# An encoder step on one Trainium2 core: the first branch product of the mix is traced in the front stage, in the buffers of h

## The chip, the cores and the metric

The kernel runs on one core of one Trainium2 chip. The metric is device time in microseconds (us) for one execution of the whole step. The core has five instruction queues that matter here: TensorE (PE, matmuls, with PEld for its weight loads), VectorE (DVE), ScalarE (ACT), GpSimd (POOL) and SyncE (SP), which issues nearly all DMA transfers. Each queue runs its instructions in order, and an instruction that waits for a semaphore holds everything behind it on the same queue.

## The reference, cut to what matters

One layer of a hybrid encoder runs for a prompt of 256 tokens and for eight samples of 16 tokens, together 384 token columns (NT). D is 1024.

```
mod = silu(c) W_ada + b_ada -> sh1, sc1, g1, sh2, sc2, g2
h   = RMSNorm(x) * (1 + sc1) + sh1
P   = h W_in  -> [RWKV-7 | sparse attention + indexer | two gates]
o_a = RWKV-7 time mixing           (16 heads of 64)
o_b = sparse attention:  q = rope(rmsnorm(q)), k = rope(rmsnorm(k)),
      indexer top-k selects keys, softmax over them, times v
gate_a, gate_b = sigmoid(P_gate + b_gate)
m   = gate_a * (o_a @ w_proj_a) + gate_b * (o_b @ w_proj_b)
x   = x + g1 * (m @ w_out)
h2  = RMSNorm(x) * (1 + sc2) + sh2
x   = x + g2 * PEER(h2)            (product keys: top 16 of 16384 experts)
```

The line that computes m is called the mix. Branch A is `gate_a * (o_a @ w_proj_a)`, branch B is the other product.

## The kernel before

All matmuls of interest take three products: an operand is split into a high and a low part (`hilo`, L230 on ACT for the high part, L234 on DVE for the low part), and high*high, low*high and high*low are added in one PSUM accumulator. A weight unit (`wload`) is two loads of 128x1024 from DRAM, each split in the same way. `tposp` then makes 24 matmuls (8 contraction steps k, 3 products) into one PSUM tile "mm" of 128x384. "mm" has two buffers.

The kernel is traced in program order, and a scheduler then puts each engine's instructions in an order of its own by a simulated timeline, with the trace order as the priority. What it writes is fixed before the run. Tiles come from pools; a tile with a tag waits for the last use of the tile that had its buffer before, and a new pool that lies on the room of a closed one waits for the old pool's last use of that room.

The stages, with their times in the profiled execution: modulation and h (to about 130 us); the front (to about 718 us), in which `ORDER` (L177) lists the units: index I, eight RWKV pairs R (R0 to R7), four attention quarters D (D0 to D3), the modulation units M (`w_ada`) and sixteen gate units G. M and G are the fill between the chains of R and D. Then come the mix (L1175), the four units of `w_out`, h2, the scores and selection of PEER (DVE does most there), and from about 1000 us to the end the dense expert stage.

The pieces that the change touches:

- RWKV pair e ends with three transposes of y (L674), a multiplication on DVE (L675, into tile sq) and a write of 128x384 to DRAM `oad[:, e]` (L676). An attention quarter u writes 128x2x384 to `obd` (L974) from a tile with the tag "qr". A gate unit writes its sigmoid to `gd` (L1164, tile gg).
- `mix` loads the products back. `parts` (L1166) makes the operands of one branch: four loads "px" of 128x768 (two buffers), each split into pbh/pbl (branch A) or pah/pal (branch B). Each branch then runs four weight units of two chunks, 192 matmuls of 128x384. Branch A's chunks are multiplied by the gate into ga (L1190), branch B's into gm, and the sum gm + ga (L1192, POOL) is split again as the operand of `w_out`.
- The pool of px lies where pools of the front lay, which are closed only after the front (`fh.close`).
- `rope` (L871) rotates pairs: two half multiplications by the sine table on POOL (L877, L878, tile rpt), one multiplication by the cosine table on DVE (L880), one addition on DVE (L881). It is called eleven times: twice in each quarter (K, then Q) and twice for the indexer's queries at 128x3x4x64, and once for the indexer's key at a quarter of that size.
- In `dsa_quarter`, K and Q are copied out of PSUM (L888, tile qx), squared on ACT (L947, into rpt), reduced on DVE (L949), turned into a reciprocal root on POOL (L436, qss), multiplied with it on DVE (L951), rotated by `rope` into kr (tag "qr"), and transposed on PE (L959).
- `attend_p` (L1063) does the prompt's part of a quarter in two halves i=0, i=1: QK and mask matmuls ("dx" accumulators), maximum on DVE (L1080), exp on ACT (L1084, tile se), transposes of it (L1092), its product with v (`dx<-vv,set`), and the transposes of the result (L1105). All its PSUM tiles have the tag "dx", which has two buffers.
- h's operand pair LTh, LTl lies in the pool hpool, one buffer each; the units that multiply with `w_in` (those of R, D and G) read it to the end of the front.

Of the kernel before, what the change touches and what calls it, by code (L numbers as in the profile page):

```python
# [13 lines left out]
F32R = mybir.dt.float32r  # L14
# [159 lines left out]

PSB = {"mm": 2, "fx": 2, "bx": 1, "dx": 2, "cp": 1}
ALIAS = {"ix": "cp", "cs": "bx", "u": "fx"}
ORDER = "GGIggggR1R23DMMMGRMRDMRGMGMRMDGMMRRMGDMMMGGGMGGM"  # L177


N1, NW, NA, NB = 40, 76, 8, 24  # L180
# [15 lines left out]
class K:  # L196
# [338 lines left out]
    def rwkv_pair(self, e):  # L535
# [137 lines left out]
        for i in range(3):  # L673
            nc.tensor.transpose(p[:, i], y[:, i], self.ident)  # L674
        nc.vector.tensor_tensor(oq, oq, p.rearrange("p i t -> p (i t)"), op=OP.mult)  # L675
        nc.sync.dma_start(self.oad[:, e], oq)  # L676
    def rwkv_inverse(self, e, MBs, MBp):


# [191 lines left out]
    def rope(self, dst, x, which, n):  # L871

        nc = self.nc
        tab = self.rt[:, which]
        B = lambda j: tab[:, :, j].unsqueeze(2).to_broadcast([128, 3, n, 32])
        t = self.t([128, 3, 4, 64], tag="rpt")[:, :, :n]
        nc.gpsimd.tensor_tensor(t[:, :, :, 0:32], x[:, :, :, 32:64], B(2), op=OP.mult)  # L877
        nc.gpsimd.tensor_tensor(t[:, :, :, 32:64], x[:, :, :, 0:32], B(3), op=OP.mult)  # L878
        cc = tab[:, :, 0:2].rearrange("p i a b -> p i (a b)").unsqueeze(2).to_broadcast([128, 3, n, 64])
        nc.vector.tensor_tensor(dst, x, cc, op=OP.mult)  # L880
        nc.vector.tensor_tensor(dst, dst, t, op=OP.add)  # L881
# [50 lines left out]
    def dsa_quarter(self, u):  # L932
        nc = self.nc
        H = lambda t: t.rearrange("p i (h d) -> p i h d", d=64)
        cols = slice(u * 256, (u + 1) * 256)
        qTs = self.t([128, 2, 8, 2, 16], tag="qTs")
        nc.gpsimd.memset(qTs, 0.0)
        qTp = self.t([128, 2, 2, 256], tag="qTp")
        for par in range(2):
            nc.gpsimd.memset(qTp[64 - 64 * par:128 - 64 * par, par], 0.0)  # L940
        kT = self.t([128, 2, NT], tag="kT")
        vn = self.t([128, 3, 256], tag="vv")
        for which, nm in ((1, "K"), (0, "Q")):
            x = self.t([128, 3, 256], tag="qx")
            self.nat3(f"{nm}{u}", x, 256)
            sq = self.t([128, 3, 256], tag="rpt")
            nc.scalar.activation(sq, x, AF.Square)  # L947
            ss = self.t([128, 3, 4], tag="qss", bufs=2)
            nc.vector.tensor_reduce(out=ss, in_=H(sq), op=OP.add, axis=AX.X)  # L949
            r = self.rstd(ss, ss, 1.0 / 64, EPS)  # L950
            nc.vector.tensor_tensor(H(x), H(x), r.unsqueeze(3).to_broadcast([128, 3, 4, 64]), op=OP.mult)  # L951
            kr = self.t([128, 3, 4, 64], tag="qr")
            self.rope(kr, H(x), 1 + which, 4)
            if which == 1:
                nc.sync.dma_start(self.O["k"][:, cols].rearrange("(i p) c -> p i c", p=128), kr.rearrange("p i a b -> p i (a b)"))
            for c in range(2):
                p = self.ps([128, 3, 128], tag="dx")
                for i in range(3):
                    nc.tensor.transpose(p[:, i], kr[:, i, 2 * c:2 * c + 2].rearrange("p a b -> p (a b)"), self.ident)  # L959
                if which == 1:  # L960
                    nc.scalar.activation(kT[:, c], p.rearrange("p i t -> p (i t)"), AF.Copy)
                else:
                    pv = p[:, 0].rearrange("p (b t) -> p b t", t=16)
                    nc.scalar.activation(qTs[0:64, c, :, 0], pv[0:64], AF.Copy)
                    nc.scalar.activation(qTs[64:128, c, :, 1], pv[64:128], AF.Copy)
                    for par in range(2):
                        pr = slice(64 * par, 64 * par + 64)
                        nc.scalar.activation(qTp[pr, par, c], p[pr, 1:3].rearrange("p i t -> p (i t)"), AF.Copy)
        self.nat3(f"V{u}", vn, 256)
        nc.sync.dma_start(self.O["v"][:, cols].rearrange("(i p) c -> p i c", p=128), vn)  # L970
        ob = self.t([128, 2, NT], tag="qr")
        self.attend_s(u, qTs, kT, vn, ob)
        self.attend_p(u, qTp, kT, vn, ob)
        nc.sync.dma_start(self.obd[:, 2 * u:2 * u + 2], ob)  # L974
    def select(self, work, rounds):

        nc = self.nc
        for _ in range(rounds):
            m8 = self.t([128, 8], tag="m8", bufs=2, pool=self.hpool)
            nc.vector.max(m8, work)  # L980
            nc.vector.match_replace(out=work, in_to_replace=m8, in_values=work, imm_value=MARK)

# [24 lines left out]
    def pick_p(self, i):  # L1007
        nc = self.nc
        n, sc = 128 * (i + 1), self.isc[1 + i]
        self.select(sc[:, :n], 8)  # L1010
        mk = self.t([128, 256], BF16, tag="mkp", bufs=2, pool=self.hpool)
        nc.vector.tensor_scalar(mk[:, :n], sc[:, :n], MARK, -BIG, op0=OP.not_equal, op1=OP.mult)
        self.mkp.append(mk)

# [34 lines left out]
    def pick_s(self):  # L1049
        nc = self.nc  # L1050
        sc = self.isc[0]
        self.select(sc, 9)
        mk = self.t([128, 384], BF16, tag="mks", pool=self.hpool)
        nc.vector.tensor_scalar(mk[:, 0:256], sc[:, 0:256], MARK, -BIG, op0=OP.not_equal, op1=OP.mult)
        m2 = self.t([128, 16], tag="m2", pool=self.hpool)
        nc.vector.tensor_scalar(m2, sc[:, 256:272], MARK, -BIG, op0=OP.not_equal, op1=OP.mult)
        ob = self.t([128, 8], tag="ob8", pool=self.hpool)
        nc.vector.tensor_scalar(ob, self.c["blk"], 1.0, BIG, op0=OP.subtract, op1=OP.mult)
        nc.vector.tensor_tensor(mk[:, 256:384].rearrange("p (b t) -> p b t", t=16), m2.unsqueeze(1).to_broadcast([128, 8, 16]),
                                ob.unsqueeze(2).to_broadcast([128, 8, 16]), op=OP.min)  # L1060
# [1 line left out]

    def attend_p(self, u, qT, kT, vn, obT):  # L1063
        nc = self.nc
        for i in range(2):
            n = 128 * (i + 1)
            nk = i + 1
# [7 lines left out]
            for par in range(2):  # L1075
# [8 lines left out]
                    nc.scalar.activation(e[:, j, :n], p[:, j, :n], AF.Exp, scale=0.125, bias=mx[:, j:j + 1],  # L1084
                                         accum_out=sm[:, 2 * j + par:2 * j + par + 1])
                es.append(e)
            pv = self.ps([128, 4, 64], tag="dx")
            for par, e in enumerate(es):
                pt = self.ps([128, 2, 2, 128], tag="dx")
                for j in range(2):  # L1090
                    for kc in range(nk):
                        nc.tensor.transpose(pt[:, j, kc], e[:, j, kc * 128:(kc + 1) * 128], self.ident)  # L1092
# [7 lines left out]
            nc.vector.reciprocal(sm, sm)  # L1100
            ob = self.t([128, 4, 64], tag="ob")
            nc.vector.tensor_tensor(ob, pv, sm.unsqueeze(2).to_broadcast([128, 4, 64]), op=OP.mult)
            p = self.ps([128, 2, 128], tag="dx")
            for c in range(2):
                nc.tensor.transpose(p[:, c], ob[:, 2 * c:2 * c + 2].rearrange("p a b -> p (a b)"), self.ident)  # L1105
            nc.scalar.activation(obT[:, :, 128 + i * 128:128 + (i + 1) * 128], p, AF.Copy)
# [52 lines left out]
    def gate_unit(self, u):  # L1159
# [3 lines left out]
        self.sigmoid(g, self.tposp(W, 0, 128, self.LT), self.hb[:, 16 + u:17 + u])  # L1163
        self.nc.sync.dma_start(self.gd[u], g)  # L1164

    def parts(self, src, tag):  # L1166
        hi = self.t([128, 8, NT], F32R, tag=tag + "h")
        lo = self.t([128, 8, NT], F32R, tag=tag + "l")
        for k in range(0, 8, 2):
            x = self.t([128, 2, NT], tag="px", bufs=2)  # L1170
            self.nc.sync.dma_start(x, src[:, k:k + 2])
            self.hilo(hi[:, k:k + 2], lo[:, k:k + 2], x)
        return hi, lo

    def mix(self):  # L1175
        nc = self.nc
        I = self.I
        gb = self.t([128, 8, NT], tag="ga")
        for br, (src, w, tg) in enumerate(((self.oad, "w_proj_a", "pb"), (self.obd, "w_proj_b", "pa"))):
            LT = self.parts(src, tg)  # L1180
            if br:
                mh, ml = self.mT = [self.t([128, 8, NT], F32R, tag=tag) for tag in ("pbh", "pbl")]
            for u in range(4):
                W = self.wload(I[w][:, u], 256)
                for c in range(2):
                    k = 2 * u + c
                    g = self.t([128, NT], tag="gm", bufs=2) if br else gb[:, k]
                    nc.sync.dma_start(g, self.gd[8 * br + k])
                    p = self.tposp(W, c, 128, LT)
                    nc.vector.tensor_tensor(g, g, p, op=OP.mult)  # L1190
                    if br:
                        nc.gpsimd.tensor_tensor(g, g, gb[:, k], op=OP.add)  # L1192
                        self.hilo(mh[:, k], ml[:, k], g, eng="v")

        self.g1 = self.t([128, 2, 1024], tag="row2")
        an = self.t([128, 3, 1024], tag="pah")
# [393 lines left out]
    def run(self):  # L1590
        hs = self.ctx.enter_context(ExitStack())
        self.halves = self.open(hs, "halves")
        with ExitStack() as front:
            fh = front.enter_context(ExitStack())
            self.fconst = self.open(fh, "fconst")
            self.hpool = self.open(fh, "hpool")
            self.fill = self.open(fh, "fill")
            self.psum = self.open(self.ctx, "psum", space=bass.MemoryType.PSUM)
            self.lo_pattern = "v"
# [10 lines left out]
                    self.setup_front()  # L1610
            self.lo_pattern = "v"
            self.gd = self.dt_([16, 128, NT])
            self.oad, self.obd = self.dt_([128, 8, NT]), self.dt_([128, 8, NT])
            with ExitStack() as s:
                rw = self.open(s, "rw")
                self.pool = rw
# [3 lines left out]
                for x in ORDER:  # L1620
# [134 lines left out]
```

## Time and profile before

| | |
|---|---|
| median of three runs | 1762.96 us (1759.18 to 1770.17) |
| the profiled execution | 1759.49 us, its span 1757.7 us |
| mean granted TensorE clock of that execution | 0.981 |
| PE busy over the span | 1679.5 us (96%) |
| DVE / ACT / POOL busy | 1353.6 / 747.5 / 550.5 us |
| front, 130 to 690 us | PE busy 541.24 of 560 us, DVE 431.33, POOL 189.59 |
| branch A's first and branch B's last matmul | about 708 and 783 us |

The engines' busy times are given by window in the prediction; a window row holds, for each engine, its busy time and the number of instructions, then the granted clock (1.00 is full), the share of the DMA engines' time and the rate. A row of the timeline holds the start, the duration, the engine, the line, the operation, the output and the inputs, and in brackets how long the engine had been idle and which instruction ended that. "SPq" is a DMA issue on SyncE; the transfer goes on after it, and the group rows give the median time from issue to landing.

### The profile page before, as it was taken

The page shows a single profiled execution, that of the slowest core. Times are in us where ns is not written, and L with a number is a line of the kernel's source. Part 1 is how long each engine was busy: PE and PEld are TensorE (multiplying, and loading weights), DVE is VectorE, ACT ScalarE, POOL GpSimd, SP SyncE. Part 2 cuts the span into 40 slices and gives each one's busy share as a digit, 9 for nine tenths or more (in the row PEclk, how much of TensorE's full clock was granted, in tenths as well). Part 3 has the DMA queues.
Part 4 walks back from the last instruction along what each step waited for, and adds up shares of the span by engine and source line. Part 5 has one row for each costly group of instructions (what it writes and reads, how often), then busy time and mean ns, then how long its engine had stood idle before and what let it go on. Part 6 is the DMA issues. An engine that isn't in the chain of part 4 may idle for free.

```text
span 1757.7 us, 33129 instructions
## 1 busy us (share of the span) xinstructions
PE 1679.5 (96%) x12392; PEld 1410.2 (80%) x12392; DVE 1353.6 (77%) x2907; ACT 747.5 (43%) x1666; POOL 550.5 (31%) x616
## 2 busy tenths in 40 slices
PE   6999899999999999999998999999999999999998
PEld 4988788777888877899887889999976667767766
DVE  4448878778867765556999998899957778778787
ACT  4533343334342333335323255578853433443344
POOL 2433343333333421024032233342243224323232
PEclk8999899999999999999999999999999999999999
DMA  8543662555365365765488999997569999999996
GB/s 305 161 123 101 187 194 68 145 166 174 94 197 161 94 207 189 246 193 171 144 334 313 358 333 366 397 340 238 179 251 381 348 346 376 375 349 391 349 379 216
DMA packets 172537, 436.71 MB, mean 248 GB/s; under 512 B 46036, under 2 KB 86100, under 8 KB 155992
## 3 DMA queue, kind: packets, MB, share of 16 engines
q1 hardware_dynamic: 153944, 300.36, 50.8%
q0 software_dynamic: 18432, 134.23, 19.7%
q8 instruction: 98, 1.61, 0.4%
q14 instruction: 63, 0.52, 0.1%
HBM read 403.23 MB, written 31.30 MB: 247 GB/s over the span
## 4 chain that ended last, share of the span: by engine, by line
PE 55%; DVE 19%; DMA 11%; issue 8%; ACT 3%; POOL 2%; SPq 1%; DVEq 0%; POOLq 0%; ACTq 0%
PE mm L226 21%; PE fx L226 10%; PE dx L226 10%; PE cp L226 6%; PE bx L226 6%; DMA raw<-in_puv,pe 3%; DVE wl L234 3%; DVE raw L1580 2%; DVE acc L1586 2%; DMA w<-in_puT 2%; DMA w<-in_pv 2%; ACT wh L230 1%; DMA w<-in_w_in 1%; DVE TX L698 1%; DMA NL<-d 1%
## 5 line engine op out<-in xcount | busy, mean ns | idle before, releaser
L234 DVE TENSOR_TENSOR wl<-w,wh 128x1024 fp32r<-128x1024 f32 (+1 forms) x276 | 345.8, 1260 | 109.0 <-ACT wh L230 71.3
L230 ACT ACTIVATE wh<-w 128x1024 fp32r<-128x1024 f32 (+1 forms) x284 | 296.6, 1050 | 163.7 <-PE mm L226 74.3
L1573 POOL DMA_INDIRECT raw<-in_puv,pe x128 | 173.6, 1356 | 423.4 <-PE dx L226 155.4
L226 PE MATMUL fx<-h2h,wl 128*128 128x256 f32 x704 | 200.1, 285 | 8.2 <-DVE wl L234 8.0
L226 PE MATMUL fx<-h2h,wh 128*128 128x256 f32 x704 | 200.6, 285 | 1.4 <-ACT wh L230 1.1
L226 PE MATMUL fx<-h2l,wh 128*128 128x256 f32 x704 | 197.4, 281 | 0.0
L1586 DVE SCALAR_TENSOR_TENSOR acc<-raw,dots,acc 128x1024 f32<-128x1024 f32 x127 | 166.1, 1308 | 14.8 <-ACT dots L1582 14.8
L1580 DVE SCALAR_TENSOR_TENSOR raw<-raw,sh 128x1024 f32<-128x1024 f32 x128 | 158.9, 1241 | 14.0 <-DMA raw<-in_puv,pe 13.8
L226 PEld LDWEIGHTS fx<-h2h,wl 128*128 128x128 f32 x704 | 132.7, 189 | 12.3 <-DVE wl L234 11.5
L226 PEld LDWEIGHTS fx<-h2h,wh 128*128 128x128 f32 x704 | 132.6, 188 | 6.4 <-ACT wh L230 3.6
L226 PEld LDWEIGHTS fx<-h2l,wh 128*128 128x128 f32 x704 | 132.9, 189 | 1.6 <-issue 1.1
L226 PE MATMUL mm<-LTh,wh 128*128 128x384 f32 (+2 forms) x352 | 123.4, 351 | 1.4 <-ACT wh L230 0.8
L226 PE MATMUL mm<-LTl,wh 128*128 128x384 f32 (+2 forms) x352 | 123.1, 350 | 0.9 <-POOL LTl L488 0.9
L226 PE MATMUL mm<-LTh,wl 128*128 128x384 f32 (+2 forms) x352 | 122.4, 348 | 0.0
L226 PE MATMUL mm<-h2f,w 128*128 128x256 f32 x448 | 104.0, 385 | 0.0
L226 PE MATMUL mm<-wh,LTh 128*128 128x256 f32 x336 | 100.3, 299 | 2.9 <-ACT qx L888 2.9
L1581 ACT ACTIVATE dots<-dots 128x1 f32<-128x1 f32 x128 | 25.6, 200 | 177.0 <-DVE raw L1580 176.5
L226 PE MATMUL mm<-wl,LTh 128*128 128x256 f32 x336 | 99.4, 296 | 0.0
L226 PE MATMUL mm<-wh,LTl 128*128 128x256 f32 x336 | 98.6, 293 | 0.0
L226 PEld LDWEIGHTS mm<-h2f,w 128*128 128x128 f32 x448 | 85.0, 192 | 12.2 <-issue 0.2
L226 PE MATMUL fx<-h2f,w 128*128 128x256 f32 x320 | 73.8, 383 | 0.0
L226 PEld LDWEIGHTS mm<-LTh,wh 128*128 128x128 f32 (+2 forms) x352 | 66.5, 189 | 7.1 <-issue 3.0
(577 smaller groups left out, 4235.0 us busy)
## 6 DMA issues: line engine op xcount, KB each, us to landing
w<-in_puT SPq DMA_DIRECT2D x128, 512.0 KB, 7.1
w<-in_pv SPq DMA_DIRECT2D x128, 512.0 KB, 6.6
w<-in_w_in SPq DMA_DIRECT2D x70, 512.0 KB, 4.5
w<-in_w_ada SPq DMA_DIRECT2D x48, 512.0 KB, 4.8
cKT<-in_cKT SPq DMA_DIRECT2D x32, 256.0 KB, 4.3
cV<-in_cV SPq DMA_DIRECT2D x32, 256.0 KB, 4.5
w<-in_w_pq SPq DMA_DIRECT2D x16, 512.0 KB, 4.2
d<-wst SPq DMA_DIRECT2D x8, 832.0 KB, 4.3
```

The lines of the kernel that those rows point to most:

```text
L226: return self.nc.tensor.matmul(out, l, r, start=start, stop=stop, skip_group_check=True, **kw)
L230: self.nc.scalar.activation(hi, src, AF.Copy)
L234: (self.nc.vector if eng == "v" else self.nc.gpsimd).tensor_tensor(lo, src, hi, op=OP.subtract)
L698: nc.vector.tensor_tensor(X[:, :t, :t], T[:, :t, :t].rearrange("p s c -> p c s"), NL[:, :t, t].unsqueeze(1).to_broadcast([48, t, t]), op=O ...
L1573: d = nc.gpsimd.indirect_dma_start(out=bass.AP(tensor=u.tensor, offset=u.offset, ap=[u.ap[0], [1, 2048]]), out_offset=None, in_=self.I["puv"],
L1580: nc.vector.scalar_tensor_tensor(u, u, 1.0, h2, op0=OP.mult, op1=OP.mult, accum_out=dot)
L1581: nc.scalar.activation(dot, dot, AF.Gelu_apprx_tanh)
L1586: nc.vector.scalar_tensor_tensor(acc, v, dot, acc, op0=OP.mult, op1=OP.add)
```

## The change: what it does

1. **Branch A moves into the front.** A new function `branch_a` is traced behind the ORDER loop, before the front's pools are closed. Its operands take the tags LTh and LTl, that is h's two buffers, so that its first split waits for the last matmul that reads h. It loads o_a in eight chunks of 128x384 ("pt", two buffers, from the RWKV pool), splits each, loads the gate chunks ("Xk", two buffers of the RWKV pool), runs the 192 matmuls, multiplies (DVE) and writes eight chunks of 192 KB to new DRAM tensors `gad`. The mix loads `gad` in place of gate A, and does branch B only.
2. **Pools.** hpool is opened outside of the front's other pools and stays open until h2 is made; the mix's sum takes LTh and LTl again instead of pbh and pbl. Small tiles of the selection (m8, mkp, mks, m2, ob8) move to fconst. `oad` and `obd` become four DRAM tensors each.
3. **ORDER's tail** goes from `DMMMGGGMGGM` to `DMGMGMGMGGM`.
4. **rope and the norm.** L878's half multiplication goes from POOL to DVE. In a quarter the square goes into kr ("qr") instead of rpt, and the multiplication by the reciprocal root comes after the rotation instead of before it.
5. **The last quarter's `attend_p`** takes its PSUM tiles pt, pv and p from the tags "fx", "cp" and "bx" instead of "dx".

```diff
-ORDER = "GGIggggR1R23DMMMGRMRDMRGMGMRMDGMMRRMGDMMMGGGMGGM"
+ORDER = "GGIggggR1R23DMMMGRMRDMRGMGMRMDGMMRRMGDMGMGMGMGGM"
...
-        nc.sync.dma_start(self.oad[:, e], oq)
+        nc.sync.dma_start(self.oad[e // 2][:, e % 2], oq)
...
         nc.gpsimd.tensor_tensor(t[:, :, :, 0:32], x[:, :, :, 32:64], B(2), op=OP.mult)
-        nc.gpsimd.tensor_tensor(t[:, :, :, 32:64], x[:, :, :, 0:32], B(3), op=OP.mult)
+        nc.vector.tensor_tensor(t[:, :, :, 32:64], x[:, :, :, 0:32], B(3), op=OP.mult)
...
-            sq = self.t([128, 3, 256], tag="rpt")
-            nc.scalar.activation(sq, x, AF.Square)
+            kr = self.t([128, 3, 4, 64], tag="qr")
+            nc.scalar.activation(kr.rearrange("p i a b -> p i (a b)"), x, AF.Square)
             ss = self.t([128, 3, 4], tag="qss", bufs=2)
-            nc.vector.tensor_reduce(out=ss, in_=H(sq), op=OP.add, axis=AX.X)
+            nc.vector.tensor_reduce(out=ss, in_=kr, op=OP.add, axis=AX.X)
             r = self.rstd(ss, ss, 1.0 / 64, EPS)
-            nc.vector.tensor_tensor(H(x), H(x), r.unsqueeze(3).to_broadcast([128, 3, 4, 64]), op=OP.mult)
-            kr = self.t([128, 3, 4, 64], tag="qr")
             self.rope(kr, H(x), 1 + which, 4)
+            nc.vector.tensor_tensor(kr, kr, r.unsqueeze(3).to_broadcast([128, 3, 4, 64]), op=OP.mult)
...
     def attend_p(self, u, qT, kT, vn, obT):
         nc = self.nc
+        tags = ("fx", "cp", "bx") if u == 3 else 3 * ("dx",)
...
+    def pair_lt(self):
+        return [self.t([128, 8, NT], F32R, tag=tag, pool=self.hpool) for tag in ("LTh", "LTl")]
+
+    def branch_a(self):
+        nc = self.nc
+        rw = self.rw
+        hi, lo = self.pair_lt()
+        for k in range(8):
+            x = self.t([128, 393], tag="pt", bufs=2, pool=rw)[:, :NT]
+            nc.sync.dma_start(x, self.oad[k // 2][:, k % 2])
+            self.hilo(hi[:, k], lo[:, k], x, "v")
+        self.gad = [self.dt_([128, NT]) for _ in range(8)]
+        for u in range(4):
+            W = self.wload(self.I["w_proj_a"][:, u], 256)
+            for c in range(2):
+                k = 2 * u + c
+                g = self.t([128, NT], tag="Xk", bufs=2, pool=rw)
+                nc.sync.dma_start(g, self.gd[k])
+                p = self.tposp(W, c, 128, (hi, lo))
+                nc.vector.tensor_tensor(g, g, p, op=OP.mult)
+                nc.sync.dma_start(self.gad[k], g)
...
+        LT = self.parts(self.obd, "pa")
+        mh, ml = self.mT = self.pair_lt()
+        for u in range(4):
+            W = self.wload(I["w_proj_b"][:, u], 256)
+            for c in range(2):
+                k = 2 * u + c
+                nc.sync.dma_start(gb[:, k], self.gad[k])
+                g = self.t([128, NT], tag="gm", bufs=2)
+                nc.sync.dma_start(g, self.gd[8 + k])
+                p = self.tposp(W, c, 128, LT)
+                nc.vector.tensor_tensor(g, g, p, op=OP.mult)
+                nc.gpsimd.tensor_tensor(g, g, gb[:, k], op=OP.add)
+                self.hilo(mh[:, k], ml[:, k], g, eng="v")
...
+            hp = front.enter_context(ExitStack())
             fh = front.enter_context(ExitStack())
+            self.hpool = self.open(hp, "hpool")
             self.fconst = self.open(fh, "fconst")
-            self.hpool = self.open(fh, "hpool")
...
                 self.nc.sync.dma_start(self.O["sh"], self.last)
+                self.branch_a()
             fh.close()
```

PE's queue at the end of the front before the change: y are R7's product (L674), se the exponentials and ob the result of the last quarter, pbh and pbl branch A's operands.

```order
L674 MATMUL bx_8139<-cfirst,y_7937 128x128 x3
L1092 MATMUL dx_8768<-cfirst,se_8756 128x128 x2
L226 MATMUL dx_8767<-vv_8202,set_8771 128x64 x2
L1092 MATMUL dx_8775<-cfirst,se_8764 128x128 x2
L226 MATMUL dx_8767<-vv_8202,set_8778 128x64 x2
L1105 MATMUL dx_8785<-cfirst,ob_8783 128x128 x2
L226 MATMUL dx_8790<-kT_8201,qTp_8198 128x256 x2
```

After the change the queue reads at the same place as follows; LTh and LTl hold branch A's operands here, and the QK matmuls of the last half (`dx<-kT,qTp`) stand ahead of these rows.

```order
L674 MATMUL bx_8139<-cfirst,y_7937 128x128 x3
L226 MATMUL cp_8765<-vv_8202,set_8769 128x64 x2
L1092 MATMUL fx_8811<-cfirst,se_8799 128x128 x4
L226 MATMUL cp_8765<-vv_8202,set_8776 128x64 x2
L1092 MATMUL fx_8822<-cfirst,se_8807 128x128 x4
L1105 MATMUL bx_8783<-cfirst,ob_8781 128x128 x2
L226 MATMUL cp_8810<-vv_8202,set_8816 128x64 x4
L226 MATMUL cp_8810<-vv_8202,set_8827 128x64 x4
L226 MATMUL mm_9153<-LTh_9097,wh_9147 128x384
L226 MATMUL mm_9182<-LTh_9097,wh_9147 128x384
L226 MATMUL mm_9153<-LTl_9098,wh_9147 128x384
L226 MATMUL mm_9153<-LTh_9097,wl_9148 128x384
```

The QK matmuls of the last half have moved ahead of R7's transposes, and 42 matmuls of branch A (steps k = 0 to 6 of two chunks) stand further up, between the last steps of R7. The last four rows begin the six matmuls of step k = 7, which reads R7's product; the other 144 matmuls of branch A follow, and behind the last of them, with nothing between, branch B's first.

SP's queue between the two branches before the change: the product of the last quarter goes to DRAM from qr, and the loads px for branch B follow it while branch A's weights are still to be read.

```order
L240 DMA w_9336<-in_w_proj_a 128x1024
L974 DMA d_410<-qr_8531 128x768
L1171 DMA px_9398<-d_410 128x768
L1171 DMA px_9402<-d_410 128x768
L412 DMA modr_9721<-in_b_ada 1x1024
```

After the change, at the boundary of the branches, d<-Xk is the write of a gated product of branch A and ga<-d the load of one.

```order
L1186 DMA d_9137<-Xk_9361 128x384
L240 DMA w_9611<-in_w_proj_b 128x1024
L1186 DMA d_9138<-Xk_9390 128x384
L240 DMA w_9681<-in_w_proj_b 128x1024
L1193 DMA px_9435<-d_413 128x768
L1193 DMA px_9439<-d_414 128x768
L1207 DMA ga_9432<-d_9131 128x384
L1209 DMA gm_9466<-d_408 128x384
```

The first loads px for branch B now stand behind the write of branch A's last product, and wait for the landing of the last writes from Xk, since px lies on Xk's room. Between the second and the third px seven loads of ga and two of gm are issued.

More of the change, by code (lines that the diff above doesn't have):

```diff
@@ L973, in dsa_quarter @@
         self.attend_p(u, qTp, kT, vn, ob)
-        nc.sync.dma_start(self.obd[:, 2 * u:2 * u + 2], ob)
+        nc.sync.dma_start(self.obd[u], ob)
     def select(self, work, rounds):
@@ L978, in select @@
         for _ in range(rounds):
-            m8 = self.t([128, 8], tag="m8", bufs=2, pool=self.hpool)
+            m8 = self.t([128, 8], tag="m8", bufs=2, pool=self.fconst)
             nc.vector.max(m8, work)
@@ L1010, in pick_p @@
         self.select(sc[:, :n], 8)
-        mk = self.t([128, 256], BF16, tag="mkp", bufs=2, pool=self.hpool)
+        mk = self.t([128, 256], BF16, tag="mkp", bufs=2, pool=self.fconst)
         nc.vector.tensor_scalar(mk[:, :n], sc[:, :n], MARK, -BIG, op0=OP.not_equal, op1=OP.mult)
@@ L1052, in pick_s @@
         self.select(sc, 9)
-        mk = self.t([128, 384], BF16, tag="mks", pool=self.hpool)
+        mk = self.t([128, 384], BF16, tag="mks", pool=self.fconst)
         nc.vector.tensor_scalar(mk[:, 0:256], sc[:, 0:256], MARK, -BIG, op0=OP.not_equal, op1=OP.mult)
-        m2 = self.t([128, 16], tag="m2", pool=self.hpool)
+        m2 = self.t([128, 16], tag="m2", pool=self.fconst)
         nc.vector.tensor_scalar(m2, sc[:, 256:272], MARK, -BIG, op0=OP.not_equal, op1=OP.mult)
-        ob = self.t([128, 8], tag="ob8", pool=self.hpool)
+        ob = self.t([128, 8], tag="ob8", pool=self.fconst)
         nc.vector.tensor_scalar(ob, self.c["blk"], 1.0, BIG, op0=OP.subtract, op1=OP.mult)
@@ L1086, in attend_p @@
                 es.append(e)
-            pv = self.ps([128, 4, 64], tag="dx")
+            pv = self.ps([128, 4, 64], tag=tags[1])
             for par, e in enumerate(es):
-                pt = self.ps([128, 2, 2, 128], tag="dx")
+                pt = self.ps([128, 2, 2, 128], tag=tags[0])
                 for j in range(2):
@@ L1102, in attend_p @@
             nc.vector.tensor_tensor(ob, pv, sm.unsqueeze(2).to_broadcast([128, 4, 64]), op=OP.mult)
-            p = self.ps([128, 2, 128], tag="dx")
+            p = self.ps([128, 2, 128], tag=tags[2])
             for c in range(2):
@@ L1170, in parts @@
             x = self.t([128, 2, NT], tag="px", bufs=2)
-            self.nc.sync.dma_start(x, src[:, k:k + 2])
+            self.nc.sync.dma_start(x, src[k // 2])
             self.hilo(hi[:, k:k + 2], lo[:, k:k + 2], x)
@@ L1178, in mix @@
         gb = self.t([128, 8, NT], tag="ga")
[L1179 to L1193, printed above, removed]
+        LT = self.parts(self.obd, "pa")
[11 more added lines that the diff above has]
+                self.hilo(mh[:, k], ml[:, k], g, eng="v")
         self.g1 = self.t([128, 2, 1024], tag="row2")
@@ L1612, in run @@
             self.gd = self.dt_([16, 128, NT])
-            self.oad, self.obd = self.dt_([128, 8, NT]), self.dt_([128, 8, NT])
+            self.oad, self.obd = ([self.dt_([128, 2, NT]) for _ in range(4)] for _ in range(2))
             with ExitStack() as s:
@@ L1648, in run @@
                     self.h2_tile(i)
+            hp.close()
         self.pool = sel
```

## The prediction

> **What bounds the kernel now.** I read the page first. PE is busy nearly all of the span, and the chain that ended last is mostly PE, with an eighth or so of transfers and a fifth of DVE:
>
> ```profile
> PE 1679.5 (96%) x12392; PEld 1410.2 (80%) x12392; DVE 1353.6 (77%) x2907; ACT 747.5 (43%) x1666; POOL 550.5 (31%) x616
> PE 55%; DVE 19%; DMA 11%; issue 8%; ACT 3%; POOL 2%; SPq 1%; DVEq 0%; POOLq 0%; ACTq 0%
> ```
>
> The change adds or removes no matmul. What it can win or lose is time in which PE stands still, or runs at a lower clock because it stood still. So the second view is the windows around the place where branch A lies, the end of the front, and the stretch of the front as a whole:
>
> ```profile
> 130.00:690.00 560.00, 541.24 (x5871) 454.24 (x5874) 431.33 (x1153) 202.28 (x483) 189.59 (x284) 0.98 0.50 151
> 650.00:690.00 40.00, 39.99 (x483) 33.79 (x485) 23.22 (x58) 15.43 (x29) 2.48 (x3) 1.00 0.69 234
> 690.00:700.00 10.00, 6.80 (x52) 5.40 (x45) 5.75 (x16) 2.99 (x13) 1.94 (x2) 0.85 0.60 227
> 700.00:710.00 10.00, 7.82 (x32) 5.33 (x32) 4.38 (x9) 4.24 (x12) 0.00 (x0) 0.67 0.52 170
> 710.00:718.60 8.60, 6.99 (x34) 6.63 (x32) 3.12 (x5) 2.91 (x4) 0.00 (x0) 0.76 0.88 337
> 718.60:783.00 64.40, 64.40 (x368) 63.92 (x369) 35.12 (x44) 25.33 (x31) 9.71 (x7) 1.00 0.60 189
> ```
>
> PE is full with fill until 690, then starves for 28.6 us, then runs the two branches without a hole: 64.40 us for 368 instructions, 0.175 us each. The third view is PE's timeline in the starved stretch:
>
> ```profile
> 693.85 0.55 PE L674 MATMUL bx<-cfirst,y 128*128 128x128 f32 x3
> ...
> 698.76 0.69 PE L1105 MATMUL dx<-cfirst,ob 128*128 128x128 f32 x2 [0.52 <-DVE ob L1102]
> ...
> 705.81 1.10 PE L226 MATMUL dx<-vv,set 128*128 128x64 f32 x8 [1.40 <-ACT se L1084]
> ...
> 708.12 0.98 PE L226 MATMUL mm<-pbh,wh 128*128 128x384 f32 x2 [0.76 <-issue]
> ...
> 709.93 0.52 PE L226 MATMUL mm<-pbh,wh 128*128 128x384 f32 x1
> 710.25 0.52 PE L226 MATMUL mm<-pbl,wh 128*128 128x384 f32 x1
> ...
> 718.59 0.44 PE L226 MATMUL mm<-pbl,wh 128*128 128x384 f32 x1 [1.61 <-DVE pbl L234]
> ```
>
> Only short chains are left there: the last pair's y, the last quarter's attention, and branch A's operands, which come late. The matmuls at 709.93 and 710.25 are 0.32 us apart, nearly twice 0.175: the clock is at half.
>
> SP and ACT show why the operands are late. The first px is issued at 703.78, 8.7 us behind the last product's write (L676):
>
> ```profile
> 695.08 0.32 SPq L676 DMA_DIRECT2D d<-sq  x1
> 703.78 0.80 SPq L1171 DMA_DIRECT2D px<-d  x2
> 704.63 3.28 SPq L1188 DMA_DIRECT2D ga<-d  x7
> 709.10 0.32 SPq L1171 DMA_DIRECT2D px<-d  x1
> ...
> 710.57 0.32 SPq L1171 DMA_DIRECT2D px<-d  x1
> ...
> 718.60 1.16 SPq L1171 DMA_DIRECT2D px<-d  x2
> 707.18 0.84 ACT L230 ACTIVATE pbh<-px 128x768 fp32r<-128x768 f32 x1 [1.42 <-DMA px<-d]
> ...
> 714.37 0.85 ACT L230 ACTIVATE pbh<-px 128x768 fp32r<-128x768 f32 x1 [5.06 <-DMA px<-d]
> ...
> 717.48 0.83 ACT L230 ACTIVATE pbh<-px 128x768 fp32r<-128x768 f32 x1
> ```
>
> From the first px to the split of the fourth and steady matmuls takes 718.59 - 703.78 = 14.8 us. Branch B's px follow at 718.60, under branch A's matmuls, and cost nothing.
>
> **The change part by part.** First, what the starved stretch costs. PE is idle 3.20 + 2.18 + 1.61 = 7.0 us in the three windows. Clocks of 0.85, 0.67 and 0.76 mean 3.0, 6.6 and 4.1 us at half speed, 13.7 us in all. PE was busy three quarters of the time (21.6 of 28.6), so half speed cost about 13.7 x 0.75 / 2 = 5.2 us, at most 6.9. Together 12 to 14 us, and I take 13.
>
> *Branch A in the front.* Of branch A, 42 matmuls (7.3 us) now stand between R7's steps. Until 690 PE had no hole for them to fill, so they push w_ada and gate work about but win nothing by themselves; what they win is that px's wait for the old pools is gone. What remains is R7's own round trip, since step k = 7 reads its product. From the transposes to the write's issue is 695.08 - 693.85 = 1.2 us. The rest is priced by these groups (the last row is that of px, L1171):
>
> ```profile
> d<-gg SPq DMA_DIRECT2D x16, 192.0 KB, 3.2
> px<-d SPq DMA_DIRECT2D x8, 384.0 KB, 4.2
> d<-sq SPq DMA_DIRECT2D x8, 192.0 KB, 1.9
> ga<-d SPq DMA_DIRECT2D x8, 192.0 KB, 4.7
> L1190 DVE TENSOR_TENSOR ga<-ga,mm x8: 554/555/556, 721.8 to 748.9; 128x384 f32<-128x384 f32 x8
> DMA to landing us min/median/max: 3.2/4.2/5.2
> ```
>
> A chunk is written in 1.9 us and read back in 1.9 to 4.7 (between the fastest 192 KB and ga<-d, which had seven others beside it; I take 3.2), then split: half of a 128x768, 0.4 us on ACT, and 0.55 on DVE as L1190. That is 1.2 + 1.9 + 3.2 + 1.0 = 7.3 us. Beside it stand the last quarter's transposes and products with v, some 4 us of PE (the QK of the last half now comes ahead, as its PSUM tags no longer share "dx"). So about 4 us of the 13 remain, 2 at best, 8 if the attention's chain of DVE and ACT steps does not overlap. Sum: -9, from -11 to -5.
>
> *The boundary of the branches.* This is new and the largest cost. Branch B's px lie on the room of Xk, so they wait until the last gated products have landed in DRAM, and PE has no other work between the branches. After branch A's last matmul come the multiplication (0.56), the issue (0.32) and the landing (1.9 as d<-sq, 3.2 as d<-gg), 2.8 to 4.1 us. Then the same pipeline runs as before at 703.78, two buffers of px, with nine loads of ga and gm between the second and third as there were seven of ga before: 14.8 us to steady matmuls. In it run those whose operands are there: 26 of branch A's 192 did before (14 and 10 and 2 around the attention), 36 if two accumulators take three of four px pairs, 4.6 to 6.3 us. The hole is 2.8 + 14.8 - 6.3 = 11.3 to 4.1 + 14.8 - 4.6 = 14.3 us. If the third px lands as fast as the quickest (3.2 us by its line, against the 5.3 from 709.10 to its split at 714.37), and ACT's fourth split follows at once, some 4 us go: 7. I take 11.5, near the row that is this same pipeline.
>
> Does the clock add to it? PE stands still for some 7 us first (2.8 + 3.4 for px, from 703.78 to 707.18, + 0.84). Before, such a start ran at half clock, but in the wait for loads slower matmuls do not set the end, and steady work at 718.60 had clock 1.00. So I add nothing. [...]
>
> *rope and the norm.* The row of waits names one stop of PE that they touch, in D0:
>
> ```profile
> PE dx L959 <- DVE qr L881: 3.4, 1, 3.4
> 191.55 3.42 POOL L877 TENSOR_TENSOR rpt<-qx,rt 128x384 f32<-128x384 f32 x1 [2.01 <-DVE qx L951]
> 194.93 1.29 POOL L878 TENSOR_TENSOR rpt<-qx,rt 128x384 f32<-128x384 f32 x1
> 196.26 1.35 DVE L881 TENSOR_TENSOR qr<-qr,rpt 128x768 f32<-128x768 f32 x1 [0.88 <-POOL rpt L878]
> 198.00:206.00 8.00, 8.00 (x53) 3.97 (x53) 5.16 (x18) 4.71 (x13) 0.61 (x1) 0.57 0.90 336
> L951 DVE TENSOR_TENSOR qx<-qx,qss 128x768 f32<-128x768 f32 x8 | 8.0, 994 | 2.2 <-POOL qss L436 2.2
> L878 POOL TENSOR_TENSOR rpt<-qx,rt 128x384 f32<-128x384 f32 x10 | 14.4, 1436 | 0.0
> ```
>
> After the root the chain was L951, L877, L878, L881: 1.0 + 3.4 + 1.3 + 1.35 = 7 us. Now only the multiplication (1.0) follows the root, with the rotation beside it. That is worth the stop of 3.4 us, and the 8 us at clock 0.57 behind it cost up to 8 x 0.43 = 3.4 more. Against it, the square now needs qr free, which the store of the K chain holds; before only the rotation did. Where that is the last wait, Q's chain grows by the square, sum and root. I take the stop and half of the clock, -5, between -7 and +3. DVE gains eleven half multiplications of 0.55 us as L1190, or 1.4 at worst as on POOL: 6 to 15 us spread over 560 in which DVE works 431. PE's queue hides that; where DVE is last in a chain, up to 1 us each time, inside the bounds given.
>
> *The rest.* ORDER's tail exchanges w_ada and gate units of fill, the same work. The eight writes of gad and the split DRAM tensors ride on DMA that is 0.60 to 0.70 busy there. Zero, and the mix's sum in LTh and LTl too: h has no reader left.
>
> Sum: -9 + 11.5 - 5 = -2.5 us on 1759.5, the profiled execution's time, 3.5 below the median of the three runs. Forecast 1757.
>
> **Rivals.**
> *The front closes its gaps.* The front's 560 us hold 18.8 us of idle PE, and its clock of 0.98 some 11 us more of half speed work lost. Half of that lies at the quarters' starts, where the shorter chain acts. If each quarter gains as D0 does, this gives -12 instead of -5; with the tail at -11 and the hole at 7 the sum is -16, or 1743. For it: the chain loses 6 us everywhere. Against it: only D0's stop is named by the rotation, and the hole's 7 needs faster loads than the rows show.
>
> *The tail does not shrink, slower.* The 42 early matmuls stand in PE's in-order queue ahead of R7's last steps. Their operands come by two buffers pt: seven chunks, each pair a read (3.2) and two splits (about 1.5), 3.5 x 4.7 = 16 us from h's last use. The work between that use and step k = 6 is about 15 us (7.3 of it theirs). If the reads take 4.7 as ga<-d, it is 22 us, PE stops for about 7 with R7 behind it, and the tail's 13 us are lost again, elsewhere. With nothing won there or in D0 and the hole at 14.3, and its end at a clock of 0.76 over 8.6 us as at 710 (8.6 x 0.24 = 2.1), the sum is +16.4, or 1776. It decides where a read takes over about 4 us.
>
> *It only moves work.* PE is bound at 96%, and if the px of branch B come earlier than the order lets me think (the write of Xk lands while other matmuls are left) and the tail keeps its chains, nothing changes: 1760.
>
> **How the numbers follow.** The forecast's bounds are -11 + 7 - 7 = -11 and -5 + 14.3 + 3 = +12: 1748 to 1772. Chances: forecast 0.56, front's gaps 0.20, tail stays 0.14, only moved 0.10. About 1% (17.6 us) is what a measurement here can tell from no change. The forecast and the last rival lie within it; the first rival lies at its edge, and I give faster by over 1% 0.18, most of that rival; slower 0.11, most of the second; within, 0.71. The range takes in the first rival's middle and half of the second: 1740 to 1775.
>
> **What would show it.** In the changed kernel: PE without a stop over 2 us between R7's transposes and the last 144 matmuls of branch A; one hole between the branches, with px named, and px issued about 3 us after the last matmul; no stop on L959's successor in D0; w_out's start shifted by as much as the whole. The forecast is wrong if the hole is under 6 us, if PE stops on the pt chunks ahead of R7's last steps, or if the time moves in the front's first three quarters by more than 7 us.

## The result: a little slower, not a little faster

The changed kernel takes 1774.34 us (median of 14 runs, 1765.83 to 1784.67), the kernel before 1764.23 us beside it. The ratio is 1.0063, with a 95% interval of 1.0047 to 1.0080: 8 to 14 us slower. That is inside the 1% that the prediction called no change, but on the other side of zero from its 2.5 us of gain. The time lies above the forecast's own bounds of 1748 to 1772 us, in part because these start from an execution 4.7 us below the median of the 14; as a difference, 10 us lies just inside its upper bound of 12. Ratios here and below leave out three executions, of 1862, 2055 and 2719 us, whose granted clock was 0.56 to 0.84 and not 0.98. The profiled execution took 1773.73 us, its span was 1771.9 us.

The page of the changed kernel shows the same picture as before, with PE's share a point lower:

```profile
span 1771.9 us, 33171 instructions
...
PE 1685.3 (95%) x12392; PEld 1407.9 (79%) x12392; DVE 1361.8 (77%) x2922; ACT 749.7 (42%) x1670; POOL 527.0 (30%) x605
...
PE 60%; DVE 16%; DMA 14%; issue 5%; ACT 3%; POOL 1%; SPq 1%; DVEq 0%; ACTq 0%; POOLq 0%
```

The windows that answer to those of before:

```profile
130.00:690.00 560.00, 546.85 (x5813) 456.76 (x5814) 426.67 (x1154) 203.73 (x484) 178.63 (x273) 0.98 0.51 155
690.00:700.00 10.00, 9.79 (x118) 8.24 (x115) 6.94 (x17) 4.74 (x11) 3.00 (x3) 1.00 0.49 165
700.00:710.00 10.00, 8.74 (x53) 6.70 (x53) 7.25 (x20) 4.04 (x17) 2.32 (x2) 1.00 0.31 100
710.00:718.60 8.60, 7.82 (x42) 7.21 (x41) 4.04 (x8) 2.23 (x4) 0.00 (x0) 0.80 0.39 122
718.60:741.20 22.60, 22.56 (x131) 22.24 (x129) 8.93 (x12) 5.50 (x6) 0.00 (x0) 1.00 0.70 233
741.20:759.00 17.80, 7.19 (x27) 6.09 (x27) 5.79 (x6) 5.00 (x8) 0.00 (x0) 0.71 0.91 297
759.00:793.00 34.00, 32.97 (x190) 32.17 (x191) 21.23 (x24) 14.30 (x20) 11.95 (x8) 1.00 0.56 171
```

The starved tail of the front is nearly gone: from 690 to 718.6 PE is idle for 2.3 us where it was 7.0. A new starved stretch stands at 741.2 to 759, between the branches. PE's timeline there, and SP's:

```profile
740.82 0.34 PE L226 MATMUL mm<-LTh,wl 128*128 128x384 f32 x1
750.12 0.98 PE L226 MATMUL mm<-pah,wh 128*128 128x384 f32 x2 [8.96 <-ACT pah L230]
...
751.92 0.52 PE L226 MATMUL mm<-pah,wh 128*128 128x384 f32 x1
752.24 0.52 PE L226 MATMUL mm<-pal,wh 128*128 128x384 f32 x1
...
754.95 0.34 PE L226 MATMUL mm<-pah,wl 128*128 128x384 f32 x1
755.13 0.33 PE L226 MATMUL mm<-pah,wh 128*128 128x384 f32 x1
...
757.96 0.61 PE L226 MATMUL mm<-pah,wh 128*128 128x384 f32 x2 [1.28 <-ACT pah L230]
758.96 0.44 PE L226 MATMUL mm<-pal,wh 128*128 128x384 f32 x1 [0.38 <-DVE pal L234]
...
773.39 0.44 PE L226 MATMUL mm<-pah,wh 128*128 128x384 f32 x1 [1.03 <-DVE gm L1211]
```

```profile
741.78 0.32 SPq L1186 DMA_DIRECT2D d<-Xk  x1
...
744.78 0.80 SPq L1193 DMA_DIRECT2D px<-d  x2
...
752.52 0.32 SPq L1193 DMA_DIRECT2D px<-d  x1
...
753.53 0.32 SPq L1193 DMA_DIRECT2D px<-d  x1
```

The last gated product is issued at 741.78, and the first px at 744.78, once that write has landed 3.0 us later. From there to steady matmuls it is 14.2 us.

Two landmarks split the difference between the two traces. Branch A's last matmul starts at 748.54 before, and at 740.82 after; branch B's last one at 782.78 before, and at 790.23 after:

```profile
748.54 0.33 PE L226 MATMUL mm<-pbh,wl 128*128 128x384 f32 x1
...
782.78 0.33 PE L226 MATMUL mm<-pah,wl 128*128 128x384 f32 x1
```

```profile
790.23 0.33 PE L226 MATMUL mm<-pah,wl 128*128 128x384 f32 x1
```

In these two traces the change wins 7.7 us up to the end of branch A; from there to the end of branch B it loses 748.54 - 740.82 + 790.23 - 782.78 = 15.2 us.

The second figure is firm. From branch A's last matmul to branch B's last one it takes 49.2 to 49.9 us in the three kernels traced with this stretch (the changed one, e3 and e4 below) and 34.2 to 35.4 us in the ten without it. The first figure is not firm: e4 runs the changed kernel's instructions in the same order, and there branch A's last matmul starts at 748.15, only 0.4 us earlier than before. What the front wins is therefore read below from the ratios of the experiments.

The other 6.7 of the 14.2 us between these two executions arise behind branch B, in stages that the change doesn't touch. From branch B's last matmul to the end it takes 974.9 us here before and 981.7 after, and over all traces between 973.5 (e9) and 984.4 (e1), so this part lies within the scatter between executions.

### The profile page after: what moved, and what is told of

Its sections match the earlier page's. It is cut to its first block, busy times and chain, and to the rows that moved or that the text cites. A ratio compares the mean times of both kernels' runs of the same rounds, so it can differ in the third digit from the quotient of the medians.

```text
span 1771.9 us, 33171 instructions
## 1 busy us (share of the span) xinstructions
PE 1685.3 (95%) x12392; PEld 1407.9 (79%) x12392; DVE 1361.8 (77%) x2922; ACT 749.7 (42%) x1670; POOL 527.0 (30%) x605
## 4 chain that ended last, share of the span: by engine, by line
PE 60%; DVE 16%; DMA 14%; issue 5%; ACT 3%; POOL 1%; SPq 1%; DVEq 0%; ACTq 0%; POOLq 0%
PE mm L226 23%; PE fx L226 11%; PE dx L226 10%; PE cp L226 7%; PE bx L226 7%; DMA raw<-in_puv,pe 3%; DMA w<-in_pv 3%; DVE wl L234 3%; DVE raw L1600 2%; DMA w<-in_puT 2%; DVE acc L1606 2%; ACT wh L230 1%; DMA w<-in_w_in 1%; DMA w<-in_w_proj_a 1%; DMA gm<-d 1%
## 5 line engine op out<-in xcount | busy, mean ns | idle before, releaser
L1593 POOL DMA_INDIRECT raw<-in_puv,pe x128 | 165.5, 1293 | 430.4 <-PE dx L226 146.6
L226 PE MATMUL mm<-LTh,wh 128*128 128x384 f32 (+2 forms) x416 | 146.6, 354 | 7.3 <-ACT gg L441 3.3
L226 PE MATMUL mm<-LTl,wh 128*128 128x384 f32 (+2 forms) x416 | 144.3, 347 | 2.1 <-DVE LTl L234 1.0
L226 PE MATMUL mm<-LTh,wl 128*128 128x384 f32 (+2 forms) x416 | 145.1, 349 | 0.0
L226 PEld LDWEIGHTS fx<-h2h,wl 128*128 128x128 f32 x704 | 132.5, 189 | 12.3 <-DVE wl L234 11.5
L226 PE MATMUL mm<-wl,LTh 128*128 128x256 f32 x432 | 126.0, 292 | 0.0
L226 PE MATMUL mm<-wh,LTl 128*128 128x256 f32 x432 | 125.5, 291 | 0.0
L226 PE MATMUL mm<-wh,LTh 128*128 128x256 f32 x432 | 125.1, 290 | 0.3 <-ACT qx L888 0.3
L226 PEld LDWEIGHTS mm<-LTh,wh 128*128 128x128 f32 (+2 forms) x416 | 79.2, 191 | 16.9 <-ACT wh L230 4.5
L226 PEld LDWEIGHTS mm<-wh,LTh 128*128 128x128 f32 x432 | 82.9, 192 | 3.0 <-issue 1.7
```

Of the source, the lines that this page charges most:

```text
L226: return self.nc.tensor.matmul(out, l, r, start=start, stop=stop, skip_group_check=True, **kw)
L1593: d = nc.gpsimd.indirect_dma_start(out=bass.AP(tensor=u.tensor, offset=u.offset, ap=[u.ap[0], [1, 2048]]), out_offset=None, in_=self.I["puv"],
```

## Experiments

All are built on the changed kernel or the kernel before, and all ratios are to the kernel before, run on the same chip. e1 to e4, e5 to e8 and e9 to e11 ran on three different chips, so a comparison of e1 with a later run is one of two ratios, and both intervals count.

### The hole between the branches

e1 puts branch A's gate chunks into two tiles of the attention's pool, which are idle by then:

```diff
             W = self.wload(self.I["w_proj_a"][:, u], 256)
+            gt = self.t([128, 2, NT], tag=("qx", "rpt")[u % 2], pool=self.ds)
             for c in range(2):
                 k = 2 * u + c
-                g = self.t([128, NT], tag="Xk", bufs=2, pool=rw)
+                g = gt[:, c]
                 nc.sync.dma_start(g, self.gd[k])
...
+                self.ds = ds
                 self.branch_a()
```

> The changed kernel, but branch A's gate chunks lie in the last quarter's idle tiles qx and rpt (on the other side of the SBUF) instead of Xk, so that the room of the RWKV pool is free once R7 is done and branch B's px can be loaded under branch A's matmuls. Theory (the hole between the branches, 741 to 759 us, is what made the change slower): the stop of 9 us and the half clock behind it go, 13 to 15 us less than the changed kernel, so 1759 to 1762 us, ratio to before 0.996 to 0.999. Rival (the loss lies in the front, spread over many short waits, and the hole only shows it): PE meets another wait in its place, ratio stays 1.004 to 1.008.

Measured: 1760.23 us, ratio 0.9963 (0.9943 to 0.9983). The windows of e1 have no hole after 720, and its SP queue issues the px at 718.61, behind R7's last chunk and under branch A's matmuls:

```profile
700.00:710.00 10.00, 9.19 (x66) 7.95 (x66) 7.79 (x20) 4.38 (x13) 4.48 (x3) 1.00 0.35 105
710.00:720.00 10.00, 8.91 (x57) 6.73 (x56) 6.26 (x16) 4.90 (x18) 0.00 (x0) 1.00 0.23 73
720.00:740.00 20.00, 20.00 (x116) 20.00 (x117) 11.82 (x14) 9.11 (x11) 0.00 (x0) 1.00 1.01 359
740.00:760.00 20.00, 20.00 (x116) 19.79 (x115) 9.95 (x13) 6.28 (x9) 3.45 (x3) 1.00 0.89 310
```

```profile
715.08 0.32 SPq L1175 DMA_DIRECT2D pt<-d  x1
718.61 0.80 SPq L1194 DMA_DIRECT2D px<-d  x2
```

The step from 1.0063 to 0.9963 is 1.0% of 1764, some 17 us (13 to 22 with both intervals), for an edit that moves small tiles. The edit also gives the gate chunks four places instead of two, but PE had no time to win by that: it was busy for 22.56 of the 22.60 us ahead of the hole. The theory holds: the hole made the change slower, and without it the change is 3 to 10 us faster than before. The rival, a loss spread over the front, falls.

e4 asks what px waits for. It allocates ga behind branch B's operands, so that px lies at addresses where no Xk tile was:

```diff
-        gb = self.t([128, 8, NT], tag="ga")
         LT = self.parts(self.obd, "pa")
+        gb = self.t([128, 8, NT], tag="ga")
```

> The changed kernel with ga allocated behind branch B's operands, so that px lies at addresses that no Xk tile has, and ga on Xk's addresses. If px's wait comes from the overlap with Xk itself, as the prediction put it, px is issued before branch A ends and the hole closes, about 1760 us. If a tile of a new pool waits for everything in the closed pool whose room it touches, px still waits for the last gated product and the time stays at 1770 to 1778 us.

Measured: one run, 1775.86 us. What decides is its trace, which has the same wait:

```profile
749.11 0.32 SPq L1186 DMA_DIRECT2D d<-Xk  x1
...
752.13 0.80 SPq L1193 DMA_DIRECT2D px<-d  x2
```

```profile
740.00:760.00 20.00, 10.85 (x55) 10.06 (x55) 7.07 (x8) 5.38 (x7) 0.00 (x0) 0.78 0.83 264
```

Again 3.0 us from the last write to px, and PE busy for only 10.85 of the 20 us. The row of SyncE's waits (line, what it waited for: us in all, times, longest us) is the same in both kernels and names the write from Xk:

```profile
SPq L1193 <- DMA d<-Xk: 1.4, 1, 1.4
```

px waits for the last use of the closed RWKV pool on whose room it lies, not only for the tiles at its own addresses. So the prediction had the wait right and its reason too narrow: moving px inside that pool's room did not mend it.

### The norm and rope edits

e2 makes only these edits in the kernel before: the half multiplication on DVE, the square in qr, the multiplication by the root behind the rotation. e3 takes them out of the changed kernel, e6 out of e1.

```diff
-            sq = self.t([128, 3, 256], tag="rpt")
-            nc.scalar.activation(sq, x, AF.Square)
+            kr = self.t([128, 3, 4, 64], tag="qr")
+            nc.scalar.activation(kr.rearrange("p i a b -> p i (a b)"), x, AF.Square)
```

> The kernel before with only the edits to rope and the norm (the half multiplication on DVE, the square in qr, the multiplication by the root behind the rotation). Theory: the stop of 3.4 us and the half clock in D0 go but Q's chain now waits for qr, so 0 to 5 us less, ratio 0.997 to 1.000. Rival (these edits cost time, because Q's square waits for the store of K): ratio 1.002 to 1.005.

> The changed kernel with rope and the norm as they were before. Theory: branch A's move costs 15 in the hole and wins 6 in the tail, so this is 9 to 13 us slower than before, ratio 1.005 to 1.008. Rival (the norm edits carry the loss): ratio 0.998 to 1.002.

> e1 with rope and the norm as before the change. Theory (the norm edits win about as much in D0 as they lose in short waits elsewhere, as the run of them alone says): within 3 us of e1, ratio 0.995 to 0.999. Rival (they win 5 us, as the prediction put it): ratio 0.999 to 1.001.

Measured: e2 1766.31 us, ratio 1.0004 (0.9983 to 1.0025); e3 1779.61 us, ratio 1.0079 (1.0048 to 1.0109); e6 1760.46 us, ratio 0.9973 (0.9958 to 0.9988). e3 and e6 lie within their theory's ranges, e2 just above its own. Alone the edits win nothing that can be measured, at most 3 us by the interval, which is short of the prediction's 5. In the changed kernel and in e1 they come out 0.0016 and 0.0010 better, 2 to 3 us, with intervals that overlap; these two comparisons alone would not rule out 5 us. Two rows of PE's waits in e2's front:

```profile
PE mm L226 <- DMA w<-in_w_ada: 5.9, 3, 4.3
...
PE dx L958 <- DVE qr L952: 0.5, 1, 0.5
```

The stop of 3.4 us on the rotation is down to 0.5 (the transposes have moved from L959 to L958), as forecast. The loads of w_ada head the list with 5.9 us, but only 1.7 us of that stands near D0: the longest stop, of 4.3 us, is at 645.27, where the kernel before stops for 2.2 us on the same loads (at 643.67). In the changed kernel the head of the list is a stop of 3.3 us at 644.65, on the tile of a gate unit:

```profile
PE mm L226 <- ACT gg L441: 3.3, 1, 3.3
```

The place of D0's old stop looks like this in the changed kernel, the last row being a window with a granted clock of 0.57:

```profile
194.49 0.64 PE L226 MATMUL mm<-w,cst 128*32 128x256 f32 x8 [1.24 <-DMA w<-in_w_ada]
196.66 0.64 PE L226 MATMUL mm<-w,cst 128*32 128x256 f32 x8 [1.52 <-DMA w<-in_w_ada]
197.71 0.75 PE L1135 MATMUL dx<-cfirst,se 128*128 128x128 f32 x3 [0.41 <-ACT se L1131]
199.00 0.69 PE L226 MATMUL mm<-LTh,wh 128*128 128x384 f32 x1 [0.55 <-ACT wh L230]
...
197.00:205.00 8.00, 7.04 (x50) 5.25 (x43) 8.00 (x19) 5.27 (x7) 2.23 (x2) 0.57 0.99 356
```

These are four stops of 3.7 us together, around the place where the one of 3.4 us was. The chain ran ahead, and PE met the next things that were late. From 170 to 200 us the stops of over 0.3 us come to 6.1 us before (1.16, 0.54, 1.01 and 3.41) and to 3.7 after, so some 2.4 us of idle time went. The half clock behind them stayed: 0.57 over 8 us, as from 198 to 206 before. The counter-term that the prediction named shows as well: in the group rows of the changed kernel's front, ACT sat idle ahead of its eight squares for 3.4 us in all until the store from qr had landed. What that cost PE is not shown.

```profile
L947 ACT ACTIVATE qr<-qx 128x768 f32<-128x768 f32 x8 | 6.7, 842 | 3.5 <-DMA d<-qr 3.4
```

### The tail: R7, the attention, the order of the fill

In the changed kernel R7's product is written at 708.05, in the kernel before at 695.08. One suspect was the load of R7's norm weights (L658), which stands at 678.97 before, and at 689.54 after behind waiting loads on SP:

```profile
688.10 0.55 SPq L240 DMA_DIRECT2D w<-in_w_proj_a  x1
689.54 1.56 SPq L658 DMA_DIRECT2D lnx<-in_rows  x2
693.26 3.91 SPq L1175 DMA_DIRECT2D pt<-d  x3
...
708.05 0.32 SPq L676 DMA_DIRECT2D d<-sq  x1
```

e5 gives that load an idle tile in e1, so that it is issued early:

```diff
-        lw = self.t([128, 2, 128], tag="lnx")
+        lw = self.t([128, 2, 128], tag="NL" if e == 7 else "lnx")
```

> e1 with one more edit: R7's group norm weights (the load lnx, L658) go to the idle tile NL, so that SyncE issues them early and not behind the waiting loads of branch A's weights and chunks. Theory (the tail gave back most of its gain because R7's product came 13 us later than before, at 708 instead of 695 us, held by that load): R7's transposes come 5 to 10 us earlier relative to the fill, and the time falls by another 2 to 5 us, ratio to before 0.993 to 0.995. Rival (PE has other work there anyway, only 2 us of idle time in e1 between 655 and 725): no change against e1, ratio 0.995 to 0.998.

Measured: 1757.97 us, ratio 0.9955 (0.9936 to 0.9974), against 0.9963 for e1. The difference is well inside the intervals, so this alone decides nothing. (The profiled execution of e5 was 13 us above its median, and its tail is not read here.)

e9 takes R7's product straight from its tile, so that the last chunk of branch A's operand needs no write, no read and no second wait:

```diff
-        nc.sync.dma_start(self.oad[e // 2][:, e % 2], oq)
+        self.oq = oq
+        if e < 7:
+            nc.sync.dma_start(self.oad[e // 2][:, e % 2], oq)
...
-            x = self.t([128, 393], tag="pt", bufs=2, pool=rw)[:, :NT]
-            nc.sync.dma_start(x, self.oad[k // 2][:, k % 2])
+            x = self.oq
+            if k < 7:
+                x = self.t([128, 393], tag="pt", bufs=2, pool=rw)[:, :NT]
+                nc.sync.dma_start(x, self.oad[k // 2][:, k % 2])
```

> e1 in which R7's product, the last chunk k = 7 of branch A's operand, is split straight from the tile it is made in, without its way through DRAM. Theory (R7's round trip of about 7 us still costs PE 4 to 8 us in the tail, as idle time, half clock and stretched matmuls): 2 to 5 us faster than e1, ratio 0.993 to 0.995. Rival (the attention's chain ends the tail anyway): same as e1, 0.995 to 0.998.

> e9 with R7's norm weights loaded early into NL as in e5. Theory (both shorten the same chain up to R7's product): 1 to 3 us faster than e9, ratio 0.992 to 0.995. Rival (R7 is no longer last): same as e9.

Measured: e9 1753.91 us, ratio 0.9947 (0.9930 to 0.9965); e10, which adds e5's edit, 1755.04 us, ratio 0.9949 (0.9929 to 0.9968). e9 has the lowest ratio of all, 6 to 12 us below the kernel before; against e1 its gain of 0.0016 (3 us) is as forecast in size, but the intervals overlap, so it is not shown. e10 wins nothing over e9 by loading the norm weights early. In its trace the load is issued at 636.66 and R7's transposes start at 709.02; in e9's they start at 706.72 with the load at 689.66. So that load was not what made R7 late. R7's product comes late in e11 below too (written at 713.68), where branch A is not in the front; what makes it late stays open. e9's windows in the tail, where e1's PE stood idle for 1.1 us between 710 and 720:

```profile
690.00:700.00 10.00, 9.78 (x124) 8.30 (x119) 7.01 (x17) 4.74 (x11) 2.94 (x3) 1.00 0.52 166
700.00:710.00 10.00, 8.84 (x56) 7.16 (x55) 7.75 (x21) 4.91 (x20) 2.37 (x2) 1.00 0.25 80
710.00:720.00 10.00, 10.00 (x67) 9.96 (x66) 6.85 (x11) 4.11 (x6) 0.00 (x0) 1.00 0.94 328
```

The one stop of over 0.3 us that is left stands at 702.25, on the split of an earlier chunk, which came by the two buffers pt:

```profile
702.25 0.44 PE L226 MATMUL mm<-LTl,wh 128*128 128x384 f32 x1 [1.02 <-DVE LTl L234]
```

e7 and e8 take ORDER's tail and the attention's PSUM tags back in e1:

```diff
-ORDER = "GGIggggR1R23DMMMGRMRDMRGMGMRMDGMMRRMGDMGMGMGMGGM"
+ORDER = "GGIggggR1R23DMMMGRMRDMRGMGMRMDGMMRRMGDMMMGGGMGGM"
```

```diff
-        tags = ("fx", "cp", "bx") if u == 3 else 3 * ("dx",)
+        tags = 3 * ("dx",)
```

> e1 with ORDER's old tail. Theory (only fill changes places): within 2 us of e1, ratio 0.995 to 0.998. Rival (the exchanged units feed the tail): 3 us or more slower than e1, ratio 0.998 or higher.

> e1 with the last quarter's PSUM tiles all under the tag dx again, so that the second half's QK waits for the first half's products. Theory (the attention's chain then stands alone beside R7's round trip): 2 to 4 us slower than e1, ratio 0.998 to 1.000. Rival (branch A's matmuls fill it): same as e1, 0.995 to 0.998.

Measured: e7 1760.48 us, ratio 0.9968 (0.9949 to 0.9987), no different from e1. e8 1762.41 us, ratio 0.9983 (0.9967 to 0.9999): 0.0020 or 3.5 us behind e1, in the middle of what the theory gave, but the intervals overlap, so it is not shown.

e11 turns it round: the kernel before with all edits but branch A's move.

> The kernel before with the norm and rope edits, ORDER's new tail and the last quarter's PSUM tags, but with both branches in the mix as before. Theory (the tags win some 3 us, norm and ORDER nothing, branch A's move with its hole costs 13): ratio 0.997 to 0.999. Rival (these edits win nothing without branch A's move): 1.000 to 1.002.

Measured: 1765.55 us, ratio 1.0004 (0.9985 to 1.0022). Without branch A beside them these edits, the attention's shorter chain among them, win nothing that can be measured; the rival holds. So nearly all of the 6.5 us that e1 wins needs branch A in the front. Whether the PSUM tags help there is left open by e8.

## Why the prediction was wrong, step by step

**What bounds the kernel.** Right as far as the runs resolve it: what they separate are stops of PE and half clock. PE's busy time rose by 5.8 us for the same 12392 matmuls, but over the traces it lies anywhere from 1675.1 (e9) to 1691.7 us (e11), so nothing follows from that.

**The tail, -9 (from -11 to -5).** Right in kind, and too large. By the prediction's own measure, idle time plus half of the busy time at half clock, 2.3 us and about 1.5 us remain of the 12 to 14 in the stretch from 690 to 718.6: the 4 us that it left. But the whole time does not show 9 us. e6 has branch A in the front, the new ORDER and the PSUM tags, and neither the hole nor the norm edits; it is 2 to 7 us faster than the kernel before, about 5. The prediction counted the whole of the tail as won and nothing as lost by pushing the fill about; where the other 4 us went stays open.

**The boundary, +11.5 (7 to 14.3).** This is the step that turned the sign. The mechanism was right and the term too small: by the landmarks the boundary cost 15.2 us, and taking it away is worth some 17. Its parts: from the last write to px 3.0 us, where the sum used 1.9 for the landing and 0.3 for the issue (DMA was 0.91 busy in that window; that this is the reason is not shown); then 14.2 us where it had 14.8; in them 26 matmuls, the lower of the two counts, where the sum took 36. From the start of branch A's last matmul to the write's issue it is 0.96 us, so the sum's own formula gives 0.96 + 3.0 + 14.2 - 4.55 = 13.6; a further 1.0 us is the stop that the gate product gm ends at 773.39, and 0.6 us is left over. The third px waited here until 752.52, 7.7 us behind the first, where it had been 5.3 us. The ends of the formula were in the text; the choice between them was made toward the cheap side without a row that favoured it.

**The clock in the hole, +0.** Right. Matmuls are 0.32 us apart at 751.92 and 0.18 again at 754.95, 4.8 us after the first one. They ran without a stop until then, and half speed was over before the next stop, of 1.28 us, which ended at 757.96. So steady work began at full speed: the granted clock was 1.00 from 759 to 793. In one point the prediction read the trace too kindly: it took the half speed at 709.93 for that of a start after some 7 us of standing still, but ahead of 709.93 no stop of PE between 690 and 710 is longer than 1.40 us.

**rope and the norm, -5 (-7 to +3).** This step failed too. The stop went, but what is late next was not asked: other stops of 3.7 us stand around the same place, and the half clock behind them stayed (0.57 over 8 us). D0 gave some 2.4 us, and in the three runs the edits came out between 0 and 3 us better.

**The sum.** -9 + 11.5 - 5 became about -5 + 15 - 2 = +8, at the lower end of the measured 8 to 14. Each of the three terms was off by some 3 to 4 us, all toward the gain, and together they turned a small gain into a loss. That the three terms were each larger than their sum was a sign that its sign was open.

**The rivals.** The front did not close its gaps (e2, e11). The tail that does not shrink is nearest in size, +16.4 against the measured +10, but that is chance: its step did not occur, for PE waited 1.0 us for a chunk (at 702.20), not 7. That the change only moves work fails by its reason: the px of branch B came late, not early, and the stall of the tail was exchanged for one at the boundary.

## What to carry to other kernels

When a phase is moved ahead of a pool's closing, look at who takes that pool's room next: here the phase's last, small tiles held the loads of the next phase until their own results had landed in DRAM, and putting them elsewhere turned 0.63% of loss into 0.37% of gain. A product that the same core needs again at once can be read from its tile and not from DRAM; e9 puts that at some 3 us here, which is not clear of the noise. And where a stop is taken away, name what is late next before its whole length is counted as gain.

## What the runs showed that was not expected

A tile of a new pool waited for the last use of the closed pool under it, even where no tile of that pool that was still in use shared an address with it (e4: px issued 3.0 us after the last write, as in the changed kernel). And the place of one and the same matmul scatters by several us between executions (branch A's last one at 740.82 in the changed kernel and at 748.15 in e4, with the same instructions in the same order), while the length of the stretch that the wait sets does not (49.4 and 49.2 us from there to branch B's last matmul).
